# Three norms of a decoder trunk: scaled rows transposed in one pass, in place of products with a diagonal

## The chip, the cores and the metric

One core of one Trainium2 chip runs the whole kernel. The metric is the device time of one execution in microseconds; the time of a kernel is the median of its runs. Inside the core, PE multiplies matrices (its weight loads are shown as PEld), VectorE (DVE) and ScalarE (ACT) work on elements, GpSimd (POOL) and the sync engine (SP) mostly start DMAs here. Each engine works through its own list of instructions in order, and waits where an operand is not ready or a buffer is not free.

## The reference

Two residual layers over x of 256 rows by 2048 columns in float32, each a mixer and a SwiGLU feed-forward network (FFN), with a modulated norm ahead of both:

```python
def rms_norm(x, gain):
    xf = x.astype(jnp.float32)
    y = xf * lax.rsqrt(jnp.mean(xf * xf, axis=-1, keepdims=True) + EPS)
    return (y * gain.astype(jnp.float32)).astype(x.dtype)

def modulate(x, shift, scale):
    return x * (1 + scale[:, None, :]) + shift[:, None, :]
...
    for layer in range(DEPTH):
        mod = silu_c @ mod_w[layer] + mod_b[layer]
        sh1, sc1, g1, sh2, sc2, g2 = jnp.split(mod, 6, axis=-1)
        h = modulate(rms_norm(x, norm_mix_gain[layer]), sh1, sc1)
        ...
        x = x + g1[:, None, :] * y
        h = modulate(rms_norm(x, norm_ffn_gain[layer]), sh2, sc2)
        x = x + g2[:, None, :] * swiglu(h, ffn_w_in[layer], ffn_w_out[layer])
```

The mixer of the first layer has eight heads of a gated recurrence (HGRN2) and eight of softmax attention with a forget gate (FoX); that of the second is gated linear attention (GLA).

## The kernel before

The 256 rows are two tiles of 128, t = 0 and 1. Every large product runs over pieces of weights (128 x 1024) that come by DMA through SP's queue. ACT rounds a piece to its upper half `hi` (L167) and VectorE takes the remainder `lo` (L169); the operand, called hT (transposed, four tiles of four column blocks of 128), is split in the same way by L356 on ACT and L357 on VectorE. PE then takes three matmuls of 512 columns for each 128 x 128 block of the operand: hi by hi (L190), hi by lo (L191), lo by hi (L192). Four `hi` and four `lo` buffers go round.

There are four norms. The first stands in the start of the kernel and is left alone. The other three stand between the stages: after the output product O of layer 0 (its tiles are named f, x_out_b), after FFN 0 (named n, the operand of the GLA projections, C), and after the output product of layer 1 (f again, x_out_c). To keep PE busy there, the last four pieces of the stage before and the first four of the stage behind are worked by row tile: all matmuls of tile 0, then all of tile 1.

As soon as tile 0 of the last product is complete, VectorE scales it by the gate (`res`, L405) and adds it to x (L406), ACT squares and sums (L315), and `norm_tile(0)` runs: `rstd_of` takes the inverse root of the mean square (three small VectorE rows, Ln and Exp on ACT at L285 and L286, one Newton step at L288 to L290). The root is multiplied into a 128 x 128 identity, `diag` (L339). Then for each of four column groups nb, PE multiplies the four 128 x 128 blocks of x by `diag` (L345): in one product a block is transposed and its rows are scaled. VectorE (two blocks, L350) and ACT (two blocks, L352) put on gain, scale and shift per column into `hm`, ACT writes the rounded upper half of hT (L356), VectorE the remainder (L357). `norm_tile(1)` does the same for tile 1 while PE multiplies tile 0 by the first four pieces of the next stage.

The order of each engine's list is not written out by hand. A scheduler orders the instructions by a simulation of the timeline; `urgently()` lifts the priority of the norm, and `issue_after(env["diag"])` keeps the first `lo` rows of the next stage behind the last diagonal.

Of the kernel before, what the change touches and what calls it, by code (L numbers as in the profile page):

```python
# [7 lines left out]
F32 = mybir.dt.float32  # L8
F32R = mybir.dt.float32r
I32 = mybir.dt.int32  # L10
AF = mybir.ActivationFunctionType
ALU = mybir.AluOpType
# [3 lines left out]
P = 128  # L16
# [50 lines left out]
def build(tc, ctx, a, out):  # L67
    nc = tc.nc
# [6 lines left out]
    env = {}  # L75

    def ps_mix(name):
        return env["pm"].tile([P, 512], F32, tag="pm", name=name)
# [7 lines left out]
    ident = const.tile([P, P], F32, name="ident")  # L86
# [233 lines left out]
    def rstd_of(ss, t, name):  # L320
        tot = small.tile([P, 1], F32, tag="sst", name=f"sst_{name}")
        r = small.tile([P, 1], F32, tag="rstd", name=f"rstd_{name}")
        nc.vector.tensor_reduce(tot, ss[:, t], op=ALU.add, axis=AX.X)
        rsqrt(r, tot, D, 1, name)
        return r
# [7 lines left out]
    def norm_tile(t):  # L333

        acol, bcol, hT, name = env["norm"]
        pool = env["pool"]
        r = rstd_of(env["ss"], t, f"{name}{t}")
        diag = pool.tile([P, P], F32, tag="diag", name=f"diag_{name}{t}", bufs=1)
        env["diag"] = nc.vector.tensor_scalar(diag, ident, r, None, ALU.mult).ins  # L339
        for nb in range(4):  # L340
            ps = ps_mix(f"xT_{name}_{nb}_{t}")
            tm = pool.tile([P, 512], F32, tag="hm", name=f"hm_{name}_{nb}_{t}", bufs=2)
            for kk in range(4):
                sl = slice(kk * P, (kk + 1) * P)
                nc.tensor.matmul(ps[:, sl], env["x"][nb][:, t, sl], diag, start=True, stop=True)  # L345
            for kk in range(4):
                kt = nb * 4 + kk
                sl = slice(kk * P, (kk + 1) * P)
                if kk < 2:
                    nc.vector.tensor_scalar(tm[:, sl], ps[:, sl], acol[:, kt:kt + 1], bcol[:, kt:kt + 1], ALU.mult, ALU.add)  # L350
                else:
                    nc.scalar.activation(tm[:, sl], ps[:, sl], AF.Identity, bias=bcol[:, kt:kt + 1], scale=acol[:, kt:kt + 1])  # L352
            hv = hT[nb][:, 0, :, t * P:(t + 1) * P]
            lv = hT[nb][:, 1, :, t * P:(t + 1) * P]
            src = tm.rearrange("p (k t) -> p k t", k=4)
            nc.scalar.copy(out=hv, in_=src)  # L356
            nc.vector.tensor_tensor(lv, src, hv, ALU.subtract)  # L357
# [817 lines left out]
    def done_out(l, nb):  # L1175
        def done(ps, t=None):
            name = f"O{l}"
            if t is None:
                residual(ps, env["x_old"], env["x"], env["row"], env["pool"], nb, name)
                sumsq(env["x"][nb], env["ss"], env["pool"], nb, f"{name}{nb}")  # L1180
                return
            if t == 0:
                assert not jobs
                start_norm(l, C_NFFN, 3, 4, f"f{l}")
            with urgently():
                residual(ps, env["x_old"], env["x"], env["row"], env["pool"], nb, name, t)
                sumsq(env["x"][nb], env["ss"], env["pool"], nb, f"{name}{nb}", (t,))
                norm_tile(t)
        return done
# [29 lines left out]
    def done_ffn_out(l, gi, nb):  # L1219
        final = gi == len(FFN_GROUPS) - 1  # L1220
        name = f"G{l}_{gi}"

        def done(ps, t=None):
            x = env["x"]
            dst = (out if l == 1 else spill)[:, nb * 512:(nb + 1) * 512]
            if t is None:
                residual(ps, x, x, env["row"], env["pool"], nb, name)
                if final:
                    if l == 0:
                        sumsq(x[nb], env["ss"], env["pool"], nb, f"{name}{nb}")  # L1230
                    nc.sync.dma_start(out=dst.rearrange("(t p) c -> p t c", p=P), in_=x[nb])
                return
            if l == 0 and t == 0:
                assert not jobs
                start_norm(1, C_NMIX, 0, 1, "n1")
            with urgently():
                residual(ps, x, x, env["row"], env["pool"], nb, name, t)
                if l == 0:
                    sumsq(x[nb], env["ss"], env["pool"], nb, f"{name}{nb}", (t,))
                    norm_tile(t)  # L1240
            nc.sync.dma_start(out=dst[t * P:(t + 1) * P], in_=x[nb][:, t])
        return done
# [176 lines left out]
```

## Time and profile before

| what | us |
|---|---|
| median of three runs | 2500.46 |
| the three runs | 2501.14, 2500.46, 2495.61 |
| the profiled execution | 2495.23 |
| its span on the core | 2493.5 |
| diagonal products at the three norms start at | 596.5, 1335.8, 1749.1 |

The profile is one execution. In the rows shown below, a group's row is line, engine, operation, output<-input, shapes, count, then busy time and mean duration in ns, then idle time of the engine ahead of them. A timeline row is start, length, engine, line, operation, and in brackets the idle time ahead of it and what ended it. A row of waits is who waited for whom, us in total, times, longest. A row of the stretches is the stretch, its length, the busy time and count of PE, PEld, DVE, ACT and POOL, then the granted PE clock, the share of the DMA engines and GB/s.

### The profile page before, as it was taken

What the parts mean: (1) busy time and instruction counts of PE and PEld (TensorE: products, weight loads), DVE (VectorE), ACT (ScalarE), POOL (GpSimd) and SP (SyncE); (2) the same over time, 40 slices, a digit from 0 to 9 for tenths busy, and PEclk for the clock granted to TensorE, in tenths of its full rate; (3) what the DMA queues carried; (4) which work ended last, traced back from release to release, by engine and by line L of the source; (5) the groups of instructions that cost most, each with busy time, mean ns of one, the idle gap of its engine ahead of it and who ended that gap; (6) DMA issues with size and microseconds to landing.
All of it is one profiled execution on the core that took longest, in us unless ns stands there. A gap on an engine that the chain in (4) does not pass through costs nothing.

```text
span 2493.5 us, 28661 instructions
## 1 busy us (share of the span) xinstructions
PE 2442.0 (98%) x11204; PEld 2002.5 (80%) x11204; DVE 1772.8 (71%) x2039; ACT 1168.8 (47%) x1625; POOL 89.6 (4%) x176
## 2 busy tenths in 40 slices
PE   7899999999999999999999999999999999999999
PEld 4578887887888888888888888888888888888887
DVE  6967887887788767767767787876776554644555
ACT  4255555545434444344345666654544344344343
POOL 0000000000000000000000000000000000000000
PEclk9999999999999999999999999999999999999999
DMA  9964767985798877777786667677486555555554
GB/s 390 420 258 168 286 253 290 347 320 215 288 367 339 318 285 285 289 286 283 286 292 208 236 246 248 250 280 260 175 313 237 188 195 189 188 191 193 190 189 148
DMA packets 93849, 647.48 MB, mean 260 GB/s; under 512 B 10417, under 2 KB 10993, under 8 KB 16401
## 3 DMA queue, kind: packets, MB, share of 16 engines
q1 hardware_dynamic: 70290, 476.59, 52.4%
q0 software_dynamic: 23424, 169.07, 18.2%
q8 instruction: 87, 1.43, 0.2%
q14 instruction: 48, 0.39, 0.0%
HBM read 641.39 MB, written 4.23 MB: 259 GB/s over the span
## 4 chain that ended last, share of the span: by engine, by line
PE 93%; DVE 4%; DMA 2%; ACT 1%; issue 1%; SPq 0%; ACTq 0%
PE acc_F L192 13%; PE acc_F L190 13%; PE acc_F L191 13%; PE acc_G L190 6%; PE acc_G L192 6%; PE acc_G L191 6%; PE acc_C L192 4%; PE acc_C L190 4%; PE acc_C L191 4%; PE acc_B L190 2%; PE acc_B L192 2%; PE acc_B L191 2%; PE acc_O L190 2%; PE acc_O L192 2%; PE acc_O L191 2%; DMA raw_s<-in_start_w_dram 2%
## 5 line engine op out<-in xcount | busy, mean ns | idle before, releaser
L169 DVE TENSOR_TENSOR lo<-raw_F,hi 128x1024 fp32r<-128x1024 f32 x352 | 429.5, 1223 | 302.3 <-ACT hi L167 302.1
L167 ACT CAST hi<-raw_F 128x1024 fp32r<-128x1024 f32 x352 | 370.6, 1054 | 478.1 <-PE acc_F L192 433.2
L192 PE MATMUL acc_F<-hi,hT_f 128*128 128x512 f32 x1408 | 551.1, 391 | 1.4 <-DVE hT_f L357 1.4
L190 PE MATMUL acc_F<-hi,hT_f 128*128 128x512 f32 x1408 | 548.7, 390 | 1.8 <-ACT hT_f L356 1.8
L191 PE MATMUL acc_F<-lo,hT_f 128*128 128x512 f32 x1408 | 548.4, 390 | 0.0
L109 DVE SCALAR_TENSOR_TENSOR mod<-mod,silu_c 128x2048 f32<-128x2048 f32 x160 | 365.3, 2284 | 4.2 <-DMA mod<-in_mod_w_dram 4.2
L169 DVE TENSOR_TENSOR lo<-raw_G,hi 128x1024 fp32r<-128x1024 f32 x176 | 214.2, 1222 | 139.3 <-ACT hi L167 139.1
L167 ACT CAST hi<-raw_G 128x1024 fp32r<-128x1024 f32 x176 | 185.4, 1055 | 268.5 <-PE acc_G L192 227.3
L192 PEld LDWEIGHTS acc_F<-hi,hT_f 128*128 128x128 f32 x1408 | 264.4, 188 | 56.9 <-DVE hT_f L357 3.0
L190 PEld LDWEIGHTS acc_F<-hi,hT_f 128*128 128x128 f32 x1408 | 264.5, 188 | 55.8 <-ACT hT_f L356 2.2
L191 PEld LDWEIGHTS acc_F<-lo,hT_f 128*128 128x128 f32 x1408 | 264.3, 188 | 55.1
L190 PE MATMUL acc_G<-hi,ct_f 128*128 128x512 f32 x704 | 273.5, 389 | 1.6 <-DVE res_G L405 1.6
L192 PE MATMUL acc_G<-hi,ct_f 128*128 128x512 f32 x704 | 274.4, 390 | 0.0
L191 PE MATMUL acc_G<-lo,ct_f 128*128 128x512 f32 x704 | 273.7, 389 | 0.0
L190 PEld LDWEIGHTS acc_G<-hi,ct_f 128*128 128x128 f32 x704 | 132.2, 188 | 29.6 <-DVE res_G L405 2.4
L191 PEld LDWEIGHTS acc_G<-lo,ct_f 128*128 128x128 f32 x704 | 132.2, 188 | 27.4
L192 PEld LDWEIGHTS acc_G<-hi,ct_f 128*128 128x128 f32 x704 | 132.2, 188 | 27.2
L190 PE MATMUL acc_C<-hi,hT_n 128*128 128x512 f32 x384 | 152.4, 399 | 0.9 <-ACT hT_n L356 0.9
L192 PE MATMUL acc_C<-hi,hT_n 128*128 128x512 f32 x384 | 151.3, 394 | 0.7 <-DVE hT_n L357 0.7
L191 PE MATMUL acc_C<-lo,hT_n 128*128 128x512 f32 x384 | 151.7, 395 | 0.0
L104 POOL DMA_DIRECT2D mod<-in_mod_w_dram x160 | 84.5, 528 | 1612.8 <-DVE mod L109 1449.8
L169 DVE TENSOR_TENSOR lo<-raw_C,hi 128x1024 fp32r<-128x1024 f32 x96 | 116.1, 1220 | 35.2 <-ACT hi L167 34.8
(343 smaller groups left out, 3399.7 us busy)
## 6 DMA issues: line engine op xcount, KB each, us to landing
raw_F<-in_ffn_w_in_dram SPq DMA_DIRECT2D x176, 1024.0 KB, 4.9
mod<-in_mod_w_dram POOLq DMA_DIRECT2D x160, 1024.0 KB, 5.2
raw_G<-in_ffn_w_out_dram SPq DMA_DIRECT2D x88, 1024.0 KB, 4.9
raw_C<-in_gla_w_in_dram SPq DMA_DIRECT2D x48, 1024.0 KB, 5.6
mod_s<-in_mod_w_dram SPq DMA_DIRECT2D x32, 1024.0 KB, 17.0
raw_B<-in_ab_w_in_dram SPq DMA_DIRECT2D x32, 1024.0 KB, 6.6
raw_s<-in_start_w_dram SPq DMA_DIRECT2D x16, 1024.0 KB, 13.9
raw_A<-in_ab_w_in_dram SPq DMA_DIRECT2D x16, 1024.0 KB, 5.0
```

What stands on the lines that cost most here:

```text
L104: nc.gpsimd.dma_start(out=tile, in_=a["mod_w"][l, part * KT + j])
L109: nc.vector.scalar_tensor_tensor(tile, tile, 1.0, silu_c, ALU.mult, ALU.mult, accum_out=modc[l, part][:, j:j + 1])
L167: nc.scalar.copy(out=hi, in_=w)
L169: env["lo"] = nc.vector.tensor_tensor(lo, w, hi, ALU.subtract)
L190: nc.tensor.matmul(o, a_hi, w_hi, start=(kt == 0), stop=False)
L191: nc.tensor.matmul(o, a_hi, w_lo, start=False, stop=False)
L192: nc.tensor.matmul(o, a_lo, w_hi, start=False, stop=(kt == last))
```

## The change

In `norm_tile` the diagonal is gone. For each column group, the 128 x 512 rows of x are multiplied by the inverse root into a new tile `xs` of two buffers, on VectorE for groups 0 and 2 and on ACT for groups 1 and 3, and PE transposes the four blocks of `xs` against the identity, in the manner of the transposes that the kernel has in other places. `env["diag"]` is now the first scaling of a tile. The rest of `norm_tile` is as it was, five lines further down.

```diff
         r = rstd_of(env["ss"], t, f"{name}{t}")
-        diag = pool.tile([P, P], F32, tag="diag", name=f"diag_{name}{t}", bufs=1)
-        env["diag"] = nc.vector.tensor_scalar(diag, ident, r, None, ALU.mult).ins
         for nb in range(4):
+            xs = pool.tile([P, 512], F32, tag="xs", name=f"xs_{name}_{nb}_{t}", bufs=2)
+            if nb % 2 == 0:
+                ins = nc.vector.tensor_scalar(xs, env["x"][nb][:, t], r, None, ALU.mult).ins
+            else:
+                nc.scalar.activation(xs, env["x"][nb][:, t], AF.Copy, scale=r)
+            if nb == 0:
+                env["diag"] = ins
             ps = ps_mix(f"xT_{name}_{nb}_{t}")
             tm = pool.tile([P, 512], F32, tag="hm", name=f"hm_{name}_{nb}_{t}", bufs=2)
             for kk in range(4):
                 sl = slice(kk * P, (kk + 1) * P)
-                nc.tensor.matmul(ps[:, sl], env["x"][nb][:, t, sl], diag, start=True, stop=True)
+                nc.tensor.transpose(ps[:, sl], xs[:, sl], ident)
```

The scheduler orders the lists anew. Outside the three norms and the stage of GLA behind the second, every engine's order is what it was; inside GLA the low-rank product and a few rows beside it stand some places earlier. At the norms the order changes in three places that matter below. The first is VectorE's list at tile 0 of the first norm, from the diagonal to the first remainder of the operand (hT_f_0). Before:

```order
L339 TENSOR_SCALAR diag_f_4534<-ident,rstd_f_4524 128x128
L169 TENSOR_TENSOR lo_4591<-raw_F_0_0_4413,hi_4590 128x1024
L169 TENSOR_TENSOR lo_4601<-raw_F_0_0_4413,hi_4600 128x1024
L169 TENSOR_TENSOR lo_4611<-raw_F_0_1_4448,hi_4610 128x1024
L405 TENSOR_TENSOR res_O_3_1_4624<-acc_O_3_4415,gate_3903 128x512
L350 TENSOR_SCALAR hm_f_0_0_4537<-xT_f_0_0_4536,acol_f_4512,modc_3_85 128x128 x2
L169 TENSOR_TENSOR lo_4621<-raw_F_0_1_4448,hi_4620 128x1024
L350 TENSOR_SCALAR hm_f_1_0_4549<-xT_f_1_0_4548,acol_f_4512,modc_3_85 128x128 x2
L406 TENSOR_TENSOR x_out_b<-xold_1_3902,res_O_3_1_4624 128x512
L357 TENSOR_TENSOR hT_f_0_4514<-hm_f_0_0_4537,hT_f_0_4514 128x4x128
```

With the change:

```order
L341 TENSOR_SCALAR xs_f_0_0_4534<-x_out_b,rstd_f_4524 128x512
L169 TENSOR_TENSOR lo_4597<-raw_F_0_0_4413,hi_4596 128x1024
L169 TENSOR_TENSOR lo_4607<-raw_F_0_0_4413,hi_4606 128x1024
L410 TENSOR_TENSOR res_O_3_1_4630<-acc_O_3_4415,gate_3903 128x512
L169 TENSOR_TENSOR lo_4617<-raw_F_0_1_4448,hi_4616 128x1024
L355 TENSOR_SCALAR hm_f_0_0_4537<-xT_f_0_0_4536,acol_f_4512,modc_3_85 128x128 x2
L341 TENSOR_SCALAR xs_f_2_0_4562<-x_out_b,rstd_f_4524 128x512
L355 TENSOR_SCALAR hm_f_1_0_4551<-xT_f_1_0_4550,acol_f_4512,modc_3_85 128x128 x2
L169 TENSOR_TENSOR lo_4627<-raw_F_0_1_4448,hi_4626 128x1024
L411 TENSOR_TENSOR x_out_b<-xold_1_3902,res_O_3_1_4630 128x512
L362 TENSOR_TENSOR hT_f_0_4514<-hm_f_0_0_4537,hT_f_0_4514 128x4x128
```

The first scaling (xs_f_0_0) takes the diagonal's place; that of group 2 (xs_f_2_0) and the second pair of hm stand ahead of the fourth lo, so one more row stands ahead of hT_f_0.

The second place is ACT's list at tile 1 of the same norm, from the Exp of the inverse root (L286) to the cast of the second column group. Before, the last pair of hm of tile 0 still stands behind Exp:

```order
L286 ACTIVATE rstd_f_4630<-rsu_f_4633 128x1
L352 ACTIVATE hm_f_3_0_4573<-xT_f_3_0_4572,modc_3_85,acol_f_4512 128x128 x2
L356 CAST hT_f_3_4517<-hm_f_3_0_4573 128x4x128
L352 ACTIVATE hm_f_0_1_4643<-xT_f_0_1_4642,modc_3_85,acol_f_4512 128x128 x2
L356 CAST hT_f_0_4514<-hm_f_0_1_4643 128x4x128
L352 ACTIVATE hm_f_1_1_4655<-xT_f_1_1_4654,modc_3_85,acol_f_4512 128x128 x2
L356 CAST hT_f_1_4515<-hm_f_1_1_4655 128x4x128
```

With the change, from the third pair of hm of tile 0:

```order
L357 ACTIVATE hm_f_2_0_4565<-xT_f_2_0_4564,modc_3_85,acol_f_4512 128x128 x2
L357 ACTIVATE hm_f_3_0_4579<-xT_f_3_0_4578,modc_3_85,acol_f_4512 128x128 x2
L285 ACTIVATE rsu_f_4639<-rsm_f_4638 128x1
L361 CAST hT_f_2_4516<-hm_f_2_0_4565 128x4x128
L361 CAST hT_f_3_4517<-hm_f_3_0_4579 128x4x128
L286 ACTIVATE rstd_f_4636<-rsu_f_4639 128x1
L343 ACTIVATE xs_f_1_1_4660<-x_out_b,rstd_f_4636 128x512
L343 ACTIVATE xs_f_3_1_4688<-x_out_b,rstd_f_4636 128x512
L357 ACTIVATE hm_f_0_1_4649<-xT_f_0_1_4648,modc_3_85,acol_f_4512 128x128 x2
L357 ACTIVATE hm_f_1_1_4663<-xT_f_1_1_4662,modc_3_85,acol_f_4512 128x128 x2
L361 CAST hT_f_0_4514<-hm_f_0_1_4649 128x4x128
L361 CAST hT_f_1_4515<-hm_f_1_1_4663 128x4x128
```

Exp now stands behind two casts and both last pairs of hm of tile 0; behind it come two scalings, then two pairs of hm in a row, and only then the two casts.

The third place is the end of the norm, on VectorE: the remainders of tile 1's groups 2 and 3 (hT_f_2, hT_f_3) among the lo rows of the next pieces. Before:

```order
L350 TENSOR_SCALAR hm_f_2_1_4667<-xT_f_2_1_4666,acol_f_4512,modc_3_85 128x128 x2
L357 TENSOR_TENSOR hT_f_1_4515<-hm_f_1_1_4655,hT_f_1_4515 128x4x128
L350 TENSOR_SCALAR hm_f_3_1_4679<-xT_f_3_1_4678,acol_f_4512,modc_3_85 128x128 x2
L169 TENSOR_TENSOR lo_4727<-raw_F_0_2_4486,hi_4726 128x1024
L357 TENSOR_TENSOR hT_f_2_4516<-hm_f_2_1_4667,hT_f_2_4516 128x4x128
L169 TENSOR_TENSOR lo_4737<-raw_F_0_2_4486,hi_4736 128x1024
L169 TENSOR_TENSOR lo_4747<-raw_F_0_3_4691,hi_4746 128x1024
L357 TENSOR_TENSOR hT_f_3_4517<-hm_f_3_1_4679,hT_f_3_4517 128x4x128
```

With the change:

```order
L355 TENSOR_SCALAR hm_f_2_1_4677<-xT_f_2_1_4676,acol_f_4512,modc_3_85 128x128 x2
L355 TENSOR_SCALAR hm_f_3_1_4691<-xT_f_3_1_4690,acol_f_4512,modc_3_85 128x128 x2
L169 TENSOR_TENSOR lo_4739<-raw_F_0_2_4486,hi_4738 128x1024
L169 TENSOR_TENSOR lo_4749<-raw_F_0_2_4486,hi_4748 128x1024
L362 TENSOR_TENSOR hT_f_2_4516<-hm_f_2_1_4677,hT_f_2_4516 128x4x128
L362 TENSOR_TENSOR hT_f_3_4517<-hm_f_3_1_4691,hT_f_3_4517 128x4x128
```

Two lo rows now stand ahead of hT_f_2, where one did, and hm of the last group has moved ahead of them.

## The prediction

> **What bounds the kernel now.** I read the page first: busy times, then the chain that ended last.
>
> ```profile
> PE 2442.0 (98%) x11204; PEld 2002.5 (80%) x11204; DVE 1772.8 (71%) x2039; ACT 1168.8 (47%) x1625; POOL 89.6 (4%) x176
> PE 93%; DVE 4%; DMA 2%; ACT 1%; issue 1%; SPq 0%; ACTq 0%
> ```
>
> PE carries 93% of the chain, so a PE pass that is taken away is worth its length wherever PE is what is late. Whether that holds at the norms is the question. The view of waits, for PE, names them:
>
> ```profile
> PE acc_F L190 <- ACT hT_f L356: 1.8, 2, 0.9
> PE acc_O L190 <- DVE res_O L405: 1.6, 2, 0.8
> PE acc_F L192 <- DVE hT_f L357: 1.4, 2, 0.7
> PE acc_C L190 <- ACT hT_n L356: 0.9, 1, 0.9
> PE acc_C L192 <- DVE hT_n L357: 0.7, 1, 0.7
> ```
>
> The three norms behave alike: 0.9 us of PE waiting for ACT's rounded operand, then 0.7 for VectorE's remainder. So one norm can be worked out and taken three times. The chain of waits around the first norm (start, length, work):
>
> ```profile
> 595.95 2.35 DVE lo L169 x2
> 598.30 0.60 DVE res_O L405
> 598.90 0.64 DVE hm_f L350 x2
> 599.60 0.99 issue
> 600.59 0.72 DVE hm_f L350 x2
> 601.31 0.60 DVE x_out_b L406
> 601.91 0.61 DVE hT_f L357
> 602.56 0.50 PE acc_F L192
> ...
> 607.85 3.57 PE xT_f L345 x32
> ```
>
> For row tile 0 VectorE is the chain from 595.95 to 602.56; the diagonal products do not stand on it. (The 0.99 called issue holds the fourth lo.) For tile 1 the products do stand on it, 3.57 us. The timeline gives the other marks:
>
> ```profile
> 594.61 0.29 DVE L339 TENSOR_SCALAR diag_f<-ident,rstd_f 128x128 f32<-128x128 f32 x1
> 595.35 1.06 ACT L167 CAST hi<-raw_F 128x1024 fp32r<-128x1024 f32 x1 [0.30 <-PE acc_O L192]
> 599.63 0.81 ACT L352 ACTIVATE hm_f<-xT_f,modc,acol_f 128x128 f32<-128x128 f32 x2 [1.88 <-DVE hm_f L350]
> 601.14 0.50 PE L190 MATMUL acc_F<-hi,hT_f 128*128 128x512 f32 x1 [0.90 <-ACT hT_f L356]
> 604.81 0.20 ACT L286 ACTIVATE rstd_f<-rsu_f 128x1 f32<-128x1 f32 x1
> 605.93 0.16 DVE L290 SCALAR_TENSOR_TENSOR rstd_f<-rsu_f,rstd_f 128x1 f32<-128x1 f32 x1
> 607.68 3.73 PE L345 MATMUL xT_f<-diag_f,x_out_b 128*128 128x128 f32 x32
> 608.77 0.73 DVE L350 TENSOR_SCALAR hm_f<-xT_f,acol_f,modc 128x128 f32<-128x128 f32 x2 [1.60 <-PE xT_f L345]
> 610.44 0.62 ACT L356 CAST hT_f<-hm_f 128x512 fp32r<-128x512 f32 x1
> 611.17 0.48 PE L190 MATMUL acc_F<-hi,hT_f 128*128 128x512 f32 x1
> 611.84 0.50 PE L192 MATMUL acc_F<-hi,hT_f 128*128 128x512 f32 x1
> 613.42 1.04 ACT L167 CAST hi<-raw_F 128x1024 fp32r<-128x1024 f32 x1
> 618.13 0.39 PE L192 MATMUL acc_F<-hi,hT_f 128*128 128x512 f32 x1
> ```
>
> Behind 611.84 PE runs without a wait; 618.13 is the 30th matmul of tile 1's restart, the first that needs tile 1's third column block complete.
>
> **What goes and what comes.** Prices, from single lines and groups:
>
> ```profile
> L345 PE MATMUL xT_f<-diag_f,x_out_b 128*128 128x128 f32 x64 | 7.5, 275 | 0.0
> L1209 PE MATMUL hT_F<-ident,fs x176: 270/272/273, 633.8 to 2449.5; 128*128 128x128 f32 x176
> L1039 DVE TENSOR_SCALAR x_s<-x_s,rstd_s x5: 479/481/486, 16.5 to 22.1; 128x512 f32<-128x512 f32 x5
> L1037 ACT ACTIVATE x_s<-x_s,rstd_s x3: 717/733/734, 20.9 to 29.7; 128x512 f32<-128x512 f32 x3
> ```
>
> A diagonal product is two passes (64 for 32 products), 7.5/64 = 0.117 us each. The FFN's transposes are 176 for 44 groups of four: one pass. So each norm loses 32 passes, 3.75 us of PE. It gains, per tile, two scalings on VectorE (0.48 each, taken from the start's own scaling of x, same shape; 0.40 until the next can start, since a 512-wide res_O shown as 0.68 takes 0.60 of the chain) in place of a diagonal of 0.29 (0.20 until the next), and two on ACT (0.73). Over three norms that is twelve more instructions on each of the two engines, less six diagonals. No DMA is added.
>
> *Tile 0.* The first scaling puts every later VectorE row back by 0.20: first hm 598.82 becomes 599.02, ACT's hm and cast follow, PE's first matmul 601.14 becomes 601.34. Then VectorE does the third block's scaling (0.40) ahead of the second hm, so the remainder (hT_f L357), on which 602.56 hangs, is 0.20 + 0.40 later: PE 603.15. ACT's scalings cost nothing here: the first sits in ACT's gap of 0.30 between the weight casts, the other in its 1.9 us of idle before hm; without that cover they would be 0.6 each. The transposes of blocks 0 and 1 run at 596.5 to 597.6; blocks 2 and 3 wait for VectorE (xs at 599.65 to 600.13), end at 601.25 and are hidden. Nothing of the shortened passes is saved. **+0.6.**
>
> *Tile 1, inverse root.* The reordered rows matter most. On VectorE both remainders, then two hm pairs follow: 602.42 + 0.60 + 0.61 + 0.73 + 0.72 = 605.1 for the last. ACT starts its fourth hm at 605.24, then 0.70 of it, 0.13 of Ln and two casts at 0.53: Exp at 607.12, where it was 604.81. VectorE then has the root at 608.48 (605.93 + 0.16 before), the scaled block 0 at 609.0. PE is through with tile 0's matmuls at 608.28, and waits 0.8.
>
> *Tile 1, blocks.* Four passes from 609.05 end at 609.67; hm 609.71 (before 608.77: only here the shorter block gives 0.47 back). xs of block 2, second hm: ends 611.46. ACT has its scaling of block 3 first, then both hm, and only then the casts: hm at 610.80 and 611.55, cast at 612.25 where it was 610.44. PE's first matmul 612.92, the third, behind the remainder, 613.64 for 611.84. **+1.8 in all.**
>
> *After it.* ACT's fifth weight cast now stands ahead of the third and fourth hm and must wait for the sixth matmul of tile 1, which frees its buffer: 614.8 for 613.42. Cast to 615.8, hm twice to 617.1, next weight cast to 618.2; on VectorE its lo (1.14) stands ahead of the remainder of block 2, done at 620.0. The 30th matmul starts at 620.06 for 618.13, with a restart of 0.1 more: **+2.1 per norm**, 6.3 for three. Behind it PE is the bound again and hands nothing back. The same bookkeeping on the present order lands within 0.15 us of each row above. If the scaling cost nothing on VectorE the norm would lose about 1.3, if it cost 0.69 like res_O about 2.9: 4 to 9 for three; I take 0.48 since it is the same operation and shape. The reordering inside the GLA layer (the low-rank product some matmuls earlier) I put at nothing: PE has no wait there, and its lists only swap neighbours; bounds -1 to +1.
>
> *The clock.* PE has gaps now of which the trace shows the price:
>
> ```profile
> 29.00:30.00 1.00, 0.14 (x2) 0.00 (x0) 0.00 (x0) 1.00 (x3) 0.00 (x0) 1.00 0.97 401
> 30.00:31.00 1.00, 0.51 (x3) 0.51 (x4) 0.00 (x0) 0.44 (x1) 0.00 (x0) 0.79 1.05 434
> 126.00:126.50 0.50, 0.17 (x1) 0.17 (x2) 0.50 (x2) 0.48 (x1) 0.00 (x0) 0.65 0.99 410
> 129.50:130.00 0.50, 0.50 (x4) 0.42 (x3) 0.50 (x3) 0.00 (x0) 0.00 (x0) 0.94 1.10 439
> 28.05 1.09 PE L1047 MATMUL xT<-ident,x_s 128*128 128x128 f32 x8 [1.35 <-ACT x_s L1037]
> 126.93 0.63 PE L1033 MATMUL acc_s<-hi_s,hT_s 128*128 128x512 f32 x1
> ```
>
> The granted clock (the third figure from the end) halves at 126.15 behind a thin stretch and returns at 129.53, 3.4 us later; at 30.6 it halves though eight transposes had run at 28.05. Meanwhile a 512-column matmul takes 0.63 in place of 0.39. After the change tile 0 leaves PE without a large matmul from 596.67 to 601.34 (4.7 us), tile 1 from 608.7 to 612.9 (4.2), and transposes for less than half of it. A 3.4 us stretch fits whole into these in (4.7 - 3.4)/3.4 = 0.4 and (4.2 - 3.4)/3.4 = 0.25 of its positions: two falls in six places. One costs up to half of 3.4, half of which the waits above hide: 0.9. I add **1.8**; bounds 0 and six falls, 5. The Trainium skill, "TensorE: Matmul & The Clock Gate", Part 4, says that transposes do not count as PE activity for the clock, and Part 1 that one idle window of about 3.4 us halves it; the fall at 30.6 behind transposes agrees. By it the diagonal products kept the clock up and the transposes do not.
>
> **The sum.** 2495.23 (the profiled execution, span 2493.5) + 6.3 + 1.8 = 2503.3. The runs shown lie in two places, 2495.6 and 2495.23 against 2500.46 and 2501.14; on the median of 2500.46 the same sum gives 2508.6. I put the forecast between the two: 2506.
>
> **Rivals.**
>
> *PE's passes come off the end.* 3 x 32 x 0.117 = 11.2 us, less restarts: 2484 to 2489, faster. For it: 93% PE in the chain, 3.57 of xT on it at tile 1. Against it: 595.95 to 602.56 is VectorE's, and scaled rows come later than the diagonal did. It decides if the first hm of tile 1 comes before 608.77. Chance 0.07.
>
> *No change that can be measured* (within 0.2%, 5 us, about what a measurement of this kernel can tell from no change). The waits are real but less than 1.67 per norm, because VectorE's scaling overlaps its neighbours more than I count and ACT's late weight casts do not reach PE: only +0.6 and about half of the +1.2 remain, 3.6 in all, no clock falls: 2499 to 2504. Chance 0.21.
>
> *The clock falls at nearly every norm tile.* Decides if a window with some matmuls in it still counts as thin (at 126.15 one matmul did not save it): 6.3 + 5 gives 2506.5 on the profiled run, 2512 on the median. Chance 0.17.
>
> *The transposes take two passes after all.* Then 16 passes more per tile at 0.117, hidden at tile 0, 0.9 at tile 1: 2.7 more, 2509. The x176 row speaks against it. Chance 0.03.
>
> The forecast, waits plus a few falls, has 0.52. Slower in all 0.72, same 0.21, faster 0.07. The range takes in the scaling's bounds (4 to 9), the clock's (0 to 5) and both places of the runs: 2499 to 2514.
>
> **What would show it.** In the profile after: xT passes 32 per norm and tile pair in place of 64; hm of tile 0 at about +0.2 and PE's wait for hT_f's remainder up from 0.7 to 1.1; a new PE wait of about 0.6 for xs at tile 1; tile 1's first hm later than before; a wait of some 0.3 at the 30th matmul; PEclk below 1.00 near some norms. I am wrong if tile 1's root comes before 607, or if PE's waits around a norm sum to no more than before while its passes fell.

## The result and the profile after

| | before | after |
|---|---|---|
| median us (lowest to highest, runs) | 2499.68 (2494.57 to 2501.14, 7) | 2507.86 (2504.27 to 2508.33, 7) |
| profiled execution us, span | 2495.23, 2493.5 | 2504.27, 2502.3 |
| mean granted clock, profiled execution | 0.997 | 0.994 |
| ratio after to before | | 1.0038 (95%: 1.0029 to 1.0047) |

The change makes the kernel 0.4% slower: 8.2 us between the medians, 8.8 between the profiled spans. The page of the profile after, busy time of each engine, then the shares of the chain that ended last:

```profile
PE 2440.6 (98%) x11108; PEld 1996.3 (80%) x11108; DVE 1774.4 (71%) x2045; ACT 1173.6 (47%) x1637; POOL 89.6 (4%) x176
PE 91%; DVE 5%; ACT 2%; DMA 1%; issue 1%; SPq 0%; ACTq 0%; DVEq 0%
```

The 96 passes are gone (11204 to 11108) and PE is busy for 1.4 us less, yet the span is longer: PE's share of the chain fell from 93% to 91%, and VectorE and ACT took it over. The view of waits of the kernel after names what PE now waits for at the norms:

```profile
PE xT_f L350 <- DVE xs_f L341: 7.0, 5, 2.7
PE xT_n L350 <- DVE xs_n L341: 4.0, 3, 2.6
PE acc_F L190 <- ACT hT_f L361: 1.8, 2, 0.9
PE acc_F L192 <- DVE hT_f L362: 1.4, 2, 0.9
PE acc_C L192 <- DVE hT_n L362: 1.1, 1, 1.1
```

The waits for the scaled rows, 11.0 us in all, are new; some 2.6 of each norm's share lies at tile 0, where PE has nothing to do in any case. What reaches the end is seen along one norm. The second one (GLA's) has no fall of the clock, so it shows the waits alone. Timeline of the kernel after, from the residual of tile 0 (`res`) to the third large matmul of tile 1:

```profile
1334.46 0.69 DVE L410 TENSOR_TENSOR res_G<-acc_G,gate 128x512 f32<-128x512 f32 x1 [1.72 <-PE acc_G L192]
1343.31 0.72 DVE L355 TENSOR_SCALAR hm_n<-xT_n,acol_n,modc 128x128 f32<-128x128 f32 x2
1344.47 1.09 PE L350 MATMUL xT_n<-ident,xs_n 128*128 128x128 f32 x8 [2.64 <-DVE xs_n L341]
1345.57 0.50 PE L190 MATMUL acc_C<-hi,hT_n 128*128 128x512 f32 x1
1347.45 0.50 PE L192 MATMUL acc_C<-hi,hT_n 128*128 128x512 f32 x1 [1.14 <-DVE hT_n L362]
1351.31 0.22 ACT L286 ACTIVATE rstd_n<-rsu_n 128x1 f32<-128x1 f32 x1
1353.27 1.09 PE L350 MATMUL xT_n<-ident,xs_n 128*128 128x128 f32 x8 [0.54 <-DVE xs_n L341]
1353.96 0.73 DVE L355 TENSOR_SCALAR hm_n<-xT_n,acol_n,modc 128x128 f32<-128x128 f32 x2 [0.75 <-PE xT_n L350]
1355.09 1.49 ACT L357 ACTIVATE hm_n<-xT_n,modc,acol_n 128x128 f32<-128x128 f32 x4
1355.14 1.09 PE L350 MATMUL xT_n<-ident,xs_n 128*128 128x128 f32 x8 [0.78 <-DVE xs_n L341]
1356.46 1.14 ACT L361 CAST hT_n<-hm_n 128x512 fp32r<-128x512 f32 x2
1357.13 0.50 PE L190 MATMUL acc_C<-hi,hT_n 128*128 128x512 f32 x1 [0.90 <-ACT hT_n L361]
1357.86 0.50 PE L192 MATMUL acc_C<-hi,hT_n 128*128 128x512 f32 x1
```

The same residual before, at the first norm:

```profile
590.17 0.69 DVE L405 TENSOR_TENSOR res_O<-acc_O,gate 128x512 f32<-128x512 f32 x1 [3.13 <-PE acc_O L192]
```

From here on a norm's **length** is the time from the start of that residual to the start of tile 1's third large matmul (L192). Before it is 611.84 - 590.17 = 21.67, the same within 0.01 at all three norms; after it is 1357.86 - 1334.46 = 23.40, so 1.73 more. In the rows one sees where: four hm of ACT stand in one row (x4) and two casts behind them (x2), so that PE's first large matmul waits 0.90 for a cast that follows two blocks' hm, and PE waited 0.54 and 0.78 before that for scaled rows.

The first and third norms also have a fall of the granted clock. Stretches of the kernel after (the third figure from the end is the clock), cut about where the clock can change (the last section says how these places were found):

```profile
599.43:602.84 3.41, 1.51 (x10) 1.15 (x10) 3.41 (x7) 2.00 (x6) 0.00 (x0) 0.99 0.93 308
602.84:606.25 3.41, 2.46 (x7) 1.57 (x6) 3.40 (x10) 2.13 (x6) 0.00 (x0) 0.50 0.61 202
606.26:609.67 3.41, 3.41 (x10) 2.65 (x9) 1.78 (x6) 2.21 (x8) 0.00 (x0) 0.51 0.25 103
1756.53:1759.94 3.41, 0.75 (x7) 0.51 (x6) 3.41 (x8) 1.97 (x5) 0.00 (x0) 1.00 0.68 197
1759.94:1763.35 3.41, 2.92 (x11) 2.11 (x9) 3.41 (x8) 2.61 (x6) 0.00 (x0) 0.50 0.55 175
```

Each fall follows a stretch in which PE was busy for less than half. At the first norm it lasts two stretches and the length is 25.16 (1.76 more than without it); at the third it lasts one and costs nothing (23.41), since PE then waits only 0.15 for the scaled rows of tile 1.

The spans' difference of 8.80 adds up along the program: 1.12 is there already at the first residual (590.17 to 591.29; the code ahead of it is untouched, and in the ten traces of this document this residual lies anywhere from 589.68 to 593.92; the clock fell there in other places, but that this makes the 1.12 is not shown); 3.88 from the first to the second residual (739.29 to 743.17: waits and one costly fall); 1.71 from the second to the third (413.32 to 415.03: waits alone); 2.09 from there to the end.

### The profile page after: what moved, and what is told of

Same layout as the page of the kernel before. It is cut to its first block, busy times and chain, and to the rows that moved or that the text cites. A ratio compares the mean times of both kernels' runs of the same rounds, so it can differ in the third digit from the quotient of the medians.

```text
span 2502.3 us, 28500 instructions
## 1 busy us (share of the span) xinstructions
PE 2440.6 (98%) x11108; PEld 1996.3 (80%) x11108; DVE 1774.4 (71%) x2045; ACT 1173.6 (47%) x1637; POOL 89.6 (4%) x176
## 4 chain that ended last, share of the span: by engine, by line
PE 91%; DVE 5%; ACT 2%; DMA 1%; issue 1%; SPq 0%; ACTq 0%; DVEq 0%
PE acc_F L192 13%; PE acc_F L191 13%; PE acc_F L190 13%; PE acc_G L190 6%; PE acc_G L192 6%; PE acc_G L191 6%; PE acc_C L190 3%; PE acc_C L191 3%; PE acc_C L192 3%; PE acc_B L190 2%; PE acc_B L191 2%; PE acc_B L192 2%; PE acc_O L190 2%; PE acc_O L192 2%; PE acc_O L191 2%; DVE mod_s L109 2%
## 5 line engine op out<-in xcount | busy, mean ns | idle before, releaser
L192 PE MATMUL acc_F<-hi,hT_f 128*128 128x512 f32 x1408 | 552.5, 392 | 1.7 <-DVE hT_f L362 1.4
L192 PEld LDWEIGHTS acc_F<-hi,hT_f 128*128 128x128 f32 x1408 | 265.2, 188 | 58.5 <-DVE hT_f L362 4.7
L192 PE MATMUL acc_G<-hi,ct_f 128*128 128x512 f32 x704 | 274.4, 390 | 0.0
L192 PEld LDWEIGHTS acc_G<-hi,ct_f 128*128 128x128 f32 x704 | 132.2, 188 | 27.2
L192 PE MATMUL acc_C<-hi,hT_n 128*128 128x512 f32 x384 | 151.7, 395 | 1.1 <-DVE hT_n L362 1.1
```

The costliest lines, as they stand in the source:

```text
L192: nc.tensor.matmul(o, a_lo, w_hi, start=False, stop=(kt == last))
```

## The experiments

All were run beside the kernel before. Lengths are of their profiled executions, in the order of the three norms; a dagger marks a fall of the clock inside it. The clock is the mean granted clock over all runs. The ratios hold the falls as well as the waits, in runs that were not traced too, so they do not follow the lengths alone (e1 against e2).

| kernel | lengths | ratio to before (95%) | clock |
|---|---|---|---|
| before | 21.67, 21.67, 21.66 | | 0.9954 (31 runs), 0.9956 (33) |
| the change | 25.16†, 23.40, 23.41† | 1.0038 (1.0029 to 1.0047) | 0.9921 |
| e1: one pass, no scaling | 22.30, 24.09†, 24.20† | 1.0019 (1.0010 to 1.0029) | 0.9940 |
| e2: scaling, two passes | 22.94, 22.97, 22.92 | 1.0010 (1.0001 to 1.0020) | 0.9965 |
| e4: the change at tile 0 | 24.74†, 22.90†, 24.85† | 1.0012 (1.0003 to 1.0022) | 0.9943 |
| e5: the change at tile 1 | 23.71†, 22.07, 22.06 | 1.0010 (1.0000 to 1.0019) | 0.9950 |
| e6: casts ahead of the next hm | 22.11, 22.34†, 22.15 | 1.0004 (0.9995 to 1.0013) | 0.9948 |
| e8: every transpose twice | 22.89, 22.94, 22.89 | 1.0006 (0.9997 to 1.0015) | 0.9965 |
| e7: tile 0's first hm on ACT | 21.05, 21.06, 21.04 | 0.9986 (0.9977 to 0.9995) | 0.9964 |
| e9: e7, and the change at tile 1 in a better order | 20.64, 20.60, 20.62 | 0.9980 (0.9971 to 0.9988) | 0.9965 |

### One pass without the scalings

This kernel leaves out the scaling of the rows by the inverse root; a constant in the column gain stands in its place.

```diff
+        nc.vector.tensor_scalar(acol, acol, 0.002, None, ALU.mult)
...
-        env["diag"] = nc.vector.tensor_scalar(diag, ident, r, None, ALU.mult).ins
+        env["diag"] = nc.vector.tensor_scalar(diag, ident, r, 0.0, ALU.mult, ALU.is_gt).ins
...
-                nc.tensor.matmul(ps[:, sl], env["x"][nb][:, t, sl], diag, start=True, stop=True)
+                nc.tensor.transpose(ps[:, sl], env["x"][nb][:, t, sl], diag)
```

> The kernel before, with each diagonal product made a one-pass transpose of the unscaled rows against a 0/1 identity that is still made from the inverse root. The scaling by the inverse root is left out (the column gain carries a constant 0.002 in its place). So it has the 32 passes of the change but none of its row scalings. Measure: from the start of the residual of VectorE at row tile 0 of a norm to tile 1's third large matmul (L192); before 21.67, after 23.40. Theory A (two causes that add: halving the passes makes the scheduler put the steps of two column blocks side by side, hm hm cast cast, on both engines, which puts tile 1's root and first cast late; and the scalings take VectorE and ACT time): here only the first is left, 22.4 to 22.5, that is +0.8 per norm, +2.4 for three, and tile 1's Exp some 1.6 later than before. Rival B (only the scalings cost): 21.2 to 21.7, the shorter block giving up to 0.47 back. Rival C (passes come off the end wherever nothing else was added): 3.7 less per norm, 18.

Timeline of this run, first norm (no fall of the clock there):

```profile
589.75 0.69 DVE L406 TENSOR_TENSOR res_O<-acc_O,gate 128x512 f32<-128x512 f32 x1 [3.13 <-PE acc_O L192]
605.98 0.20 ACT L286 ACTIVATE rstd_f<-rsu_f 128x1 f32<-128x1 f32 x1
609.27 1.50 ACT L353 ACTIVATE hm_f<-xT_f,modc,acol_f 128x128 f32<-128x128 f32 x4 [3.08 <-PE xT_f L346]
610.65 1.15 ACT L357 CAST hT_f<-hm_f 128x512 fp32r<-128x512 f32 x2
611.33 0.50 PE L190 MATMUL acc_F<-hi,hT_f 128*128 128x512 f32 x1 [1.64 <-ACT hT_f L357]
612.05 0.50 PE L192 MATMUL acc_F<-hi,hT_f 128*128 128x512 f32 x1
```

22.30, 0.63 more than before (I had put down 0.8), although PE's passes are halved and no scaling is added. Exp comes at 605.98 - 589.75 = 16.23 behind the residual where it was 14.64, and the four hm stand ahead of the two casts. The passes saved do not shorten the norm; the shorter blocks make the scheduler put two column blocks side by side. That speaks against both rivals: PE's passes do not come off the end, and the scalings are not the whole loss.

### The scalings with two passes

```diff
-                nc.tensor.transpose(ps[:, sl], xs[:, sl], ident)
+                nc.tensor.matmul(ps[:, sl], xs[:, sl], ident, start=True, stop=True)
```

> The changed kernel with its transposes written as ordinary products of the scaled rows with the identity (two passes, 64 per norm as before). The scalings stay; on VectorE and ACT the steps stand block by block again, as before. Theory A (order and scalings both cost): 22.7 to 22.8 from the residual to tile 1's third large matmul, +1.1 per norm, +3.3 for three: less than the change although PE does twice the passes. Rival B (only the scalings cost): not less than the change's 23.4, plus up to 0.47 for the longer block, 23.4 to 23.9. For the clock: if it falls because transposes do not hold it up, no fall at the norms here and a mean granted clock of 0.997 as before; if it falls because PE waits, falls at tile 0 as in the change (0.992).

```profile
589.68 0.69 DVE L410 TENSOR_TENSOR res_O<-acc_O,gate 128x512 f32<-128x512 f32 x1 [3.13 <-PE acc_O L192]
610.04 2.27 PE L350 MATMUL xT_f<-ident,xs_f 128*128 128x128 f32 x16 [0.32 <-DVE xs_f L341]
612.62 0.40 PE L192 MATMUL acc_F<-hi,hT_f 128*128 128x512 f32 x1
```

These are timeline rows of the first norm. 22.94: with twice the passes the norm is 0.46 shorter than the change's, because the steps stand block by block again. It is 0.2 longer than I expected; the PE wait of 0.32 for the third block's scaled rows is a wait I had not counted here. No clock falls at any norm, and the mean clock is above that of the change in every run (0.996 to 0.997 against 0.991 to 0.994).

### The change at one tile

In the first of these two kernels tile 1, in the second tile 0, keeps the diagonal and its products:

```diff
+            if t == 0:
                 xs = pool.tile([P, 512], F32, tag="xs", name=f"xs_{name}_{nb}_{t}", bufs=2)
...
+                if t == 0:
+                    nc.tensor.transpose(ps[:, sl], xs[:, sl], ident)
+                else:
+                    nc.tensor.matmul(ps[:, sl], env["x"][nb][:, t, sl], diag, start=True, stop=True)
```

> The change at row tile 0 of each norm alone; tile 1 keeps the diagonal and its two-pass products. Theory A: tile 0 pays its 0.6 and the paired order puts tile 1's root at 607.1 in the first norm's times, as in the change, but tile 1's own steps stand block by block: 22.9 to 23.0 from the residual to the third large matmul, +1.3 per norm, +3.9 for three. Rival B (only the scalings cost, each tile by its own): about +0.6, 22.3. Rival D (the loss is made at tile 1): no more than +0.2. Clock: falls at tile 0 (after the first norm's residual by 5 to 18 us) are possible as in the change.

> The change at row tile 1 of each norm alone; tile 0 keeps the diagonal and its products. Theory A: the root of tile 1 comes as early as before, the first hm 0.4 earlier than before, but ACT does both its scalings and two hm pairs ahead of the first cast: 22.1 from the residual to the third large matmul, +0.45 per norm, +1.4 for three, hardly to be told from before in the time. Rival B (scalings cost by themselves, wherever they are): +1.0 or more. Rival C (passes come off where PE is the bound, as at tile 1): 21.2 or less, faster by 0.5 to 1.8 per norm. Clock: no falls at tile 0.

Timeline rows of the second norm, of the first kernel and then of the second, from the residual to tile 1's third large matmul; in the second, L290 ends the inverse root of tile 1:

```profile
1336.24 0.69 DVE L417 TENSOR_TENSOR res_G<-acc_G,gate 128x512 f32<-128x512 f32 x1 [1.72 <-PE acc_G L192]
1359.14 0.50 PE L192 MATMUL acc_C<-hi,hT_n 128*128 128x512 f32 x1
```

```profile
1332.63 0.69 DVE L417 TENSOR_TENSOR res_G<-acc_G,gate 128x512 f32<-128x512 f32 x1 [1.72 <-PE acc_G L192]
1348.40 0.16 DVE L290 SCALAR_TENSOR_TENSOR rstd_n<-rsu_n,rstd_n 128x1 f32<-128x1 f32 x1
1350.17 1.03 PE L355 MATMUL xT_n<-ident,xs_n 128*128 128x128 f32 x8
1354.70 0.50 PE L192 MATMUL acc_C<-hi,hT_n 128*128 128x512 f32 x1
```

22.90 (second norm; the fall there lasts one stretch and costs nothing to be seen against the 22.9 to 23.0 expected) and 22.07: +1.23 from tile 0, +0.40 from tile 1, together 1.63 of the change's 1.73. Most of the loss is made at tile 0, where the transposes themselves are hidden: what tile 0 does there is to put tile 1's root late. At tile 1 the first scalings hide, as the root (15.93 behind the residual) comes 1.6 us before PE is free (17.54); for the scaled rows of the third block PE waits 0.78. That the shorter block gives back some of what the pairing costs there is likely, but no run divides the 0.40. The fall at e5's first norm (at 603.0, tile 0) was not expected: tile 0 is as before there, so the kernel before can fall at this place too. It lasts one stretch and costs 1.64, as PE waits for nothing while it lasts. A second fall of one stretch begins at 613.2, with tile 1's first large matmuls, so that most of it lies behind the length.

### Casts ahead of the next block's hm

```diff
-                    nc.scalar.activation(tm[:, sl], ps[:, sl], AF.Identity, bias=bcol[:, kt:kt + 1], scale=acol[:, kt:kt + 1])
+                    with tc.issue_after(cast.ins) if nb else ExitStack():
+                        nc.scalar.activation(tm[:, sl], ps[:, sl], AF.Identity, bias=bcol[:, kt:kt + 1], scale=acol[:, kt:kt + 1])
...
-            nc.scalar.copy(out=hv, in_=src)
+            cast = nc.scalar.copy(out=hv, in_=src)
```

> The changed kernel, with one order added: ACT's half of a column block's hm is issued behind the cast of the block before it. The scalings, the one-pass transposes and the passes stay. Theory A (order and scalings add): the pairs are gone, tile 1's Exp comes about 0.5 earlier, its first cast stands behind one hm and not two, and the remainders behind the casts: 22.1 from the residual to tile 1's third large matmul where no clock falls (the change 23.40, before 21.67). Rival (the pairing is only a symptom, the scalings make the whole loss): 23.2 to 23.5. Clock: falls at tile 0 as in the change, 1.8 each where they last two windows, so that the time is 2502 to 2504.

```profile
591.57 0.69 DVE L411 TENSOR_TENSOR res_O<-acc_O,gate 128x512 f32<-128x512 f32 x1 [3.13 <-PE acc_O L192]
607.63 0.19 ACT L286 ACTIVATE rstd_f<-rsu_f 128x1 f32<-128x1 f32 x1
611.46 0.79 ACT L358 ACTIVATE hm_f<-xT_f,modc,acol_f 128x128 f32<-128x128 f32 x2
612.28 0.62 ACT L362 CAST hT_f<-hm_f 128x512 fp32r<-128x512 f32 x1
613.68 0.50 PE L192 MATMUL acc_F<-hi,hT_f 128*128 128x512 f32 x1
```

Timeline of the first norm: hm x2, then the cast, in place of x4 and x2. 22.11 as expected, 1.29 less than the change with the same scalings and the same passes. So the pairing is a cause by itself and no symptom: with the scalings in place 1.29 of the 1.73 hang on it. What is left, 0.44, should be the scalings' time less what the shorter block gives; no run divides it. These are not fixed shares, for the parts overlap: the order without the scalings cost 0.63 (e1), the scalings without the paired order and with two passes 1.27 (e2). The time, 2499.89, is better than the 2502 to 2504 that I expected, as the profile has only one fall at the norms, of one stretch (and one ahead of them, at 546.1).

### Every transpose twice

```diff
                 nc.tensor.transpose(ps[:, sl], xs[:, sl], ident)
+                nc.tensor.transpose(ps[:, sl], xs[:, sl], ident)
```

> The changed kernel with every transpose between the stages made twice into the same place: PE has as many passes as with the diagonal products (64 per norm) and the instructions of all engines stand in the order of the run with two-pass products of the scaled rows, so only the kind of the passes differs from that run (22.93 without a fall, no fall at any norm, mean granted clock 0.996 to 0.997). Theory C1 (transposes do not keep the granted clock up, products do): 22.9 where no clock falls, but falls at tile 0 of one to three norms, mean clocks of 0.991 to 0.995, time 2501 to 2505. Rival C2 (any passes keep it up; what counts is how long PE is busy): no falls, clocks of 0.996 to 0.997, time 2499 to 2500.

Stretches of this run, then one of e1 and one of e4, each with the stretch behind it:

```profile
598.79:602.20 3.41, 1.62 (x15) 1.38 (x14) 3.41 (x6) 2.16 (x4) 0.00 (x0) 1.00 0.86 286
602.20:605.61 3.41, 2.88 (x17) 2.17 (x15) 3.27 (x9) 2.82 (x8) 0.00 (x0) 1.00 0.76 259
```

```profile
596.43:599.84 3.41, 1.58 (x15) 1.34 (x13) 3.41 (x8) 1.55 (x3) 0.00 (x0) 1.00 0.59 171
599.84:603.25 3.41, 1.83 (x7) 1.22 (x8) 3.41 (x6) 2.53 (x7) 0.00 (x0) 1.00 0.70 228
```

```profile
1342.62:1346.03 3.41, 1.02 (x9) 0.78 (x7) 3.41 (x6) 1.92 (x4) 0.00 (x0) 1.00 0.46 127
1346.03:1349.44 3.41, 3.01 (x11) 2.29 (x12) 3.41 (x7) 3.26 (x8) 0.00 (x0) 0.50 0.69 204
```

In the first two pairs all of the 15 matmuls of the first stretch are transposes, 1.62 and 1.58 us of PE, and the clock stays at 1.00 behind them. In the third, eight transposes and the end of a matmul make 1.02 us, and it falls. The lengths (22.89 to 22.94) and the mean clock (0.9965) are those of e2, whose passes are products. So rival C2 holds here: a transpose keeps the clock up as a product of the same length does, and how long PE is busy in the stretch counts. It does not settle every case: behind stretches with large matmuls of 1.8 us of PE (e5) and 1.94 (e6) the clock fell. The times fit a price of the halved passes: e6's norms are 0.6 to 0.8 shorter than e8's, and its time is no better (2499.89 against 2499.53), with a mean clock of 0.9948 against 0.9965. But these 2 us lie within the intervals, so the times alone do not show it.

### Two kernels that are faster than before

The wait at tile 0 in the kernel before hangs on VectorE while ACT idles 1.88, so the first takes VectorE's two hm of tile 0's first block to ACT:

```diff
-                if kk < 2:
+                if kk < (0 if nb == 0 and t == 0 else 2):
```

> The kernel before, with all four hm of row tile 0's first column block on ACT, where two were on VectorE. ACT was idle for 1.9 there, VectorE was the chain. If VectorE is what sets tile 0's start: first large matmul of tile 0 up to 1 earlier, the one behind the remainder 0.6 earlier, and tile 1 follows: 21.0 from the residual to tile 1's third large matmul for 21.67, about 1.9 less for three norms, hardly to be told in the time (ratio 0.9992). Rival: tile 1 is set by ACT's casts and the root, which come no earlier, and all of it is lost there: 21.6.

The second adds the change at tile 1 alone, with three `xs` buffers (the diagonal of tile 0 uses one of them), the scalings of groups 0, 2 and 3 on VectorE, and e6's order at tile 1:

```diff
+            if t != 0:
+                xs = pool.tile([P, 512], F32, tag="xs", name=f"xs_{name}_{nb}_{t}", bufs=3)
+                if nb != 1:
+                    ins = nc.vector.tensor_scalar(xs, env["x"][nb][:, t], r, None, ALU.mult).ins
+                else:
+                    nc.scalar.activation(xs, env["x"][nb][:, t], AF.Copy, scale=r)
```

> The kernel before, with all four hm of tile 0's first block on ACT, and at row tile 1 alone the change's scaled rows and one-pass transposes, with three buffers for them, three of the four scalings on VectorE, and each hm of ACT behind the cast of the block before. At tile 1 the root comes 2 us before PE is free, so a scaling can hide there. Theory A: 20.6 from the residual to tile 1's third large matmul, 1.1 less than before per norm, 3.2 for three, ratio 0.9987, as long as no clock falls are added at tile 1. Rival B (each scaling costs its time): 21.0 to 21.7. Rival D (PE's gap at tile 1 makes the clock fall): as A but with falls some 20 us behind the residual and no gain in the time.

Timeline of the second kernel's first norm:

```profile
590.96 0.69 DVE L418 TENSOR_TENSOR res_O<-acc_O,gate 128x512 f32<-128x512 f32 x1 [3.13 <-PE acc_O L192]
598.47 1.50 ACT L365 ACTIVATE hm_f<-xT_f,modc,acol_f 128x128 f32<-128x128 f32 x4
602.74 0.50 PE L192 MATMUL acc_F<-hi,hT_f 128*128 128x512 f32 x1 [1.22 <-DVE hT_f L370]
606.30 0.88 DVE L345 TENSOR_SCALAR xs_f<-x_out_b,rstd_f 128x512 f32<-128x512 f32 x2
607.91 1.47 PE L355 MATMUL xT_f<-ident,xs_f 128*128 128x128 f32 x12
611.60 0.50 PE L192 MATMUL acc_F<-hi,hT_f 128*128 128x512 f32 x1
```

The lengths came as expected, 21.05 and 20.62 on average; three times 0.62 and 1.05 of 2498 are ratios of 0.9993 and 0.9987. The measured ones, 0.9986 and 0.9980, are lower, but their intervals take these in. In the second kernel the scalings at 606.30 lie ahead of the moment when PE is free, and PE starts the transposes of three blocks at 607.91 without a wait (for the fourth it waits 0.35). Which part of the new order earns the 0.43 between the two kernels is not divided. Neither profile has a fall at a norm. Both kernels are faster than before, by 0.1 to 0.2%, and so than the change; which of the two is the faster, the intervals leave open.

## Why the prediction was right, point by point

The forecast was 2506, 2503.3 on the profiled execution and 2508.6 on the median; measured were 2504.27 and 2507.86. Times below are distances from the residual, before (first norm) and after (second norm).

- **Tile 0, +0.6.** First hm of VectorE 8.65 to 8.85 (+0.20, as said), the matmul behind the remainder 12.39 to 12.99 (+0.60). The wait for the remainder is 1.14 (1.1 said).
- **Tile 1, root late.** Exp 14.64 to 16.85, +2.21 (said +2.31); the transposes start +1.30 later, behind a wait of 0.54 (0.8 in the working, 0.6 among the signs). Shown as a cause of its own by e1, where Exp moved by 1.59 without any scaling, and by e4.
- **Tile 1, blocks, "+1.8 in all".** First hm +0.90 (said +0.94), third matmul +1.73. Pinning the order gives 1.29 of it back (e6), and 0.44 is left with the scalings and the shorter block.
- **After it, "+2.1 per norm, 6.3 for three".** This term is a little too large. The prediction's own rows give 620.06 - 618.13 + 0.1, 2.03 per norm and 6.1 for three. At the third norm the 30th matmul comes 0.51 behind the 29th where others come 0.23 behind each other, so it waits 0.28 (29.94 for 27.93, +2.0), as its rows show; but at the second its operand is in time and the loss stays at 1.73. About 2.0 + 1.7 + 2.0 = 5.7 for three.

```profile
1778.92 0.39 PE L191 MATMUL acc_F<-lo,hT_f 128*128 128x512 f32 x1
1779.43 0.50 PE L192 MATMUL acc_F<-hi,hT_f 128*128 128x512 f32 x1
```

- **GLA's reordering at nothing.** Right: the stage from the second to the third norm is longer by 1.71, which is its norm's own 1.73.
- **The clock, +1.8 from two falls of 0.9.** In the profiled execution two of the six places fell and together cost 1.76, but not as 0.9 each, so the match of the total is luck. A fall of two stretches cost 1.76 here and 1.8 to 1.95 in e1 and e4. One of a single stretch costs what PE's waits do not take up: nothing at the third norm here, 0.2 in e6, 1.64 in e5. The reason that I took along was wrong: by the Trainium skill, "TensorE: Matmul & The Clock Gate", Part 4, transposes do not count as PE-busy in the same way, and I let the fall at 30.6 speak for it. e8 and e1 contradict it: stretches with nothing but transposes kept the clock. The fall at 30.6 came behind a stretch with 1.17 us of PE, which is short enough by itself. That the products kept the clock up before because they took twice as long fits the trace before, where the thinnest stretch at each norm holds 2.18 to 2.52 us of PE, and e8.
- **The sum.** Waits of 5.7 and 8.2 between the medians leave 2.5, for the clock as far as is known; I had 6.3 and 1.8. The two errors offset each other, which is luck. In the profiled spans the 8.80 are 5.7 of waits, 1.76 of falls, the 1.12 ahead of the first norm, for which the sum had no term, and 0.2 more. The other six runs of the change have a clock of 0.991 or 0.992, below the profiled one's 0.994, so they had more or longer falls, at the norms or elsewhere; which places they hit is not seen, as only one execution was traced.

The rivals: *PE's passes come off the end* fell with e1. *No change* needed half of tile 1's loss to vanish; it is all there. *Falls at nearly every tile* did not happen in the profile, and the clock of the other runs leaves it partly open. *Two passes* fell with the count of 32 per norm.

## What to carry to other kernels

A pass taken from the engine with 98% busy time is worth little where that engine is about to wait: of the 3.75 us of passes that the change takes from a norm, e6 against e2 gets at most 0.83. At the norms the question was when the root and the first cast come, and that was set by VectorE's and ACT's lists. A scheduler that orders by its own estimates will reorder these lists when an operation elsewhere gets shorter; compare the lists, and if a chain lost its order, pin it (one `issue_after` gave back 1.29 of 1.73). New work on a neighbour engine is free only where it ends before the consumer is free, as the first scalings at tile 1 do, and not at tile 0, where VectorE is what PE waits for.

## What the hardware showed that was not expected

The granted clock moves on a grid of 3.413 us that runs through the whole program and lies differently in every execution: the falls of one trace start at whole multiples of it from each other (in the profile after 39.6, 602.8 and 1759.9: the later two 165 and 504 steps behind the first). In the ten traces, behind the first 20 us, every stretch of the grid in which PE was busy for less than 1.4 us was followed by a halved clock, those from 1.4 to 1.95 went both ways, and none above fell. A halved clock came back behind stretches with about 2.9 us or more of work; at that edge it went both ways (2.88 came back, 2.94 once did not). A kernel like this one, with the same code, differs by several microseconds from run to run (before: 2494.57 to 2501.14), and the granted clock goes with it: of the 31 runs beside e1 to e5, the three with 0.994 took 2500.2 to 2502.3 and the five with 0.997 2495.3 to 2496.5. That where the grid falls on the thin places decides this is likely, but only one execution of each kernel was traced.
